# A decoder layer on one core: every stage laid out as [channel, token], norms summed over partitions, one address offset for matrix operands

## The chip, the cores and the metric

The kernel runs on 1 core of one Trainium2 chip. The metric is the device time of one execution in microseconds (us), median of the runs.

## What is computed

One layer (DEPTH 1), 1024 tokens, width 1024, float32:

```python
h = rmsnorm(x, g_mix); z = h @ w_in                 # 1024 x 7168, seven sections
y_rnn  = gelu(rnn_y) * rg_lru(causal_conv4(rnn_x))  # recurrence over the tokens
y_conv = conv_b * causal_conv3(conv_c * conv_x)
x = x + (sigmoid(gate_rnn) * y_rnn + sigmoid(gate_conv) * y_conv) @ w_out
g, u = split(rmsnorm(x, g_ffn) @ w_gate_up); x = x + (silu(g) * u) @ w_down   # inner width 2816
x = x + sigmoid(rmsnorm(x, g_ple) @ w_ple_gate) * (p @ w_ple)
return rmsnorm(x, g_final)
```

## The kernel before, in words

Each float32 operand of a product is kept as two halves (hi, lo) of 12 bits, and each 128x128 by 128x512 block takes three float32r matmuls. The large products use Strassen's scheme: seven products of quarter matrices, numbered 1 to 7, in place of eight. `mm` (L108) issues the three matmuls, `split` (L83) makes the halves: ScalarE casts (L85), VectorE subtracts (L86).

The stages, in order. **Start** (to 44 us): p @ w_ple in `ple` (L474), which stores `pe_d`, and the norm of x. **First stream** (to 638 us): the input projection as 28 pairs of channel blocks, with the recurrence (`rg` matmuls) and the convolutions. **Output projection** (`outer`, L336, to 716 us): product with w_out, added to x (`acc`, L433, line L435), stored as `x2_d`, normed. **Second stream** (to 1140 us): gate and up in 22 pairs. **Down projection** (to 1357 us): `outer` three times, added to x, stored as `x3_d`, normed. **Gate stage** (to the end): `gate` (L860) per block of 128 tokens, final norm, output.

A *stream* (L207) has channels on the partitions and tokens on the free axis. Its weights arrive as `part` tiles and become `wop` tiles (cast L250, subtraction L254) in pools `wp` (5 tiles) and `wq` (2); two products of each seven take `wq`. In a matmul `wop` is the loaded side (weights) and an operand made from the norm the moving side. There are seven such operands, B11, B21, T1, T2, B22, T3, -T4, of which B11 and B21 come from the first 512 tokens alone and the others from both halves. The first eight products use B11 and B21 only (`LEAD = 4` pairs); then the order is T2, T1, T3, T2, B22, T1, -T4.

Around the norms x is [token, channel], one tile per 128 tokens. `squares` (L115) lets ScalarE square a tile and sum along the free axis; `rstd` (L121) is a chain of small operations; rows are scaled (L144 on VectorE, L146 on ScalarE), and `transposed` (L148) turns each 128x128 block on TensorE (`tp`, L151), 64 blocks for each of the three norms. The reader of the bank applies the gain (L167, L169, L190, L192):

```python
def right_operands(r11, r21, xt, ss, gc, piece, held=0):
    ...
    scale_rows(xt, rstd(ss, 4), True)
    ...
            ps = transposed(xt, kk)
            t = r11[k // 2][:, k % 2]
            nc.vector.scalar_tensor_tensor(out=t, in0=ps, scalar=col(gc + kk), in1=t,
                                           op0=ALU.mult, op1=ALU.subtract)
            nc.scalar.activation(q[k // 2][:, k % 2], ps, AF.Copy, scale=col(gc + kk))
```

`r_late` tiles (L415) take the memory of the first half's x. Order on each engine is made at build time from priorities; `high_priority` and `sooner` move instructions forward, a negative offset back.

Memory, in bytes per partition, each tile rounded up to 32: constants `cp` 512 + 448 + 32 + 32 = 1024, then `ops` (seven operands of 16384), then `sm` (small tiles of the norms, 704 in all), then the pools of the stage. In a stream these are `w1`, `w2`, `ws` (multiples of 2048), `wp`, then `ev`, `e0` and behind them `wq`. `e0` holds four tiles of 512 floats in the second stream and of 516 in the first. In the gate stage half of one left operand lies in the place of x tiles (`op_in_x`, L845).

Of the kernel before, what the change touches and what calls it, by code (L numbers as in the profile page):

```python
# [25 lines left out]
# columns of the per-channel constants  # L26
C_W4, C_B4, C_BR, C_BI, C_LAM, C_W3, C_GM, C_GF, C_GP, NCST = 0, 32, 40, 48, 56, 64, 88, 96, 104, 112

# sections of the input projection
# [6 lines left out]
def kernel(ctx, tc, x, pT, w_in, w_gu, w_rg, w_out, w_down, w_pg, w_ple, cst, g_fin, out):  # L36
# [12 lines left out]
"""  # L49
# [12 lines left out]
    x2_d = tc.dram_tile([T, D], F32, name="x2_d")  # L62
    x3_d = tc.dram_tile([T, D], F32, name="x3_d")
    pe_d = tc.dram_tile([T, D], F32, name="pe_d")
# [8 lines left out]
    ident = cp.tile([P, P], F32, name="ident")  # L73
    make_identity(nc, ident)
    cs = cp.tile([P, NCST], F32, name="cs")
# [7 lines left out]
    def split(hi, lo, src):  # L83
        """hi + lo == src, each with 12 significant bits."""
        nc.scalar.copy(hi, src)  # L85
        nc.vector.tensor_sub(lo, src, hi.bitcast(F32))  # L86

    def op_of(pieces, name):
        """A quarter of a matrix, given as pieces [P, k, H], as an operand."""
        t = ops.tile([P, 2, 4, H], F32R, tag="op", name=name)  # L90
        k = 0
        for q in pieces:
            n = q.shape[1]
            split(t[:, 0, k:k + n], t[:, 1, k:k + n], q)
            k += n
        return t
# [18 lines left out]
    def squares(ss, n, piece, jp):  # L115
        junk = jp.tile([P, D], BF16, tag="junk", name="junk", bufs=1)
        nc.scalar.activation(junk[:, :piece.shape[1]], piece, AF.Square, accum_out=ss[:, n:n + 1])

    root = [None]  # the last square root, behind which other tables may be loaded

    def rstd(ss, nb):  # L121
        """(sum of the parts / D + EPS) ** -0.5, with one Newton step behind the table."""
        v = sm.tile([P, nb], F32, name="rv")
        total = ss[:, 0:nb]
        for n in range(nb, ss.shape[1], nb):
            add(v, total, ss[:, n:n + nb])
            total = v
# [12 lines left out]
    def scale_rows(xt, y, spread):  # L140
        """xt[b] *= y[:, b]; spread: VectorE takes its share."""
        for b in range(4):
            if spread:
                nc.vector.tensor_scalar_mul(xt[b], xt[b], y[:, b:b + 1])  # L144
            else:
                nc.scalar.activation(xt[b], xt[b], AF.Copy, scale=y[:, b:b + 1])  # L146

    def transposed(xt, kk):  # L148
        ps = bank("tp")
        for b in range(4):  # L150
            nc.tensor.transpose(ps[:, b * P:(b + 1) * P], xt[b][:, kk * P:(kk + 1) * P], ident)  # L151
        return ps

    def norm_half(xt, ss, gc, piece, spread):
# [3 lines left out]
        scale_rows(xt, rstd(ss, 4), spread)  # L158
        quarters = []
        for kh in range(2):  # L160
            q = [piece(), piece()]
            for k in range(4):
                kk = 4 * kh + k
                ps = transposed(xt, kk)
                dst = q[k // 2][:, k % 2]
                if spread and k % 2:
                    nc.vector.tensor_scalar_mul(dst, ps, col(gc + kk))  # L167
                else:
                    nc.scalar.activation(dst, ps, AF.Copy, scale=col(gc + kk))  # L169
# [3 lines left out]
    def right_operands(r11, r21, xt, ss, gc, piece, held=0):  # L173
# [4 lines left out]
        o = [op_of(r11, "b11"), op_of(r21, "b21")]  # L178
# [3 lines left out]
        scale_rows(xt, rstd(ss, 4), True)  # L182
        second = []
        for kh in range(2):
            q = [piece(), piece()]
            for k in range(4):
                kk = 4 * kh + k
                ps = transposed(xt, kk)
                t = r11[k // 2][:, k % 2]
                nc.vector.scalar_tensor_tensor(out=t, in0=ps, scalar=col(gc + kk), in1=t,  # L190
                                               op0=ALU.mult, op1=ALU.subtract)
                nc.scalar.activation(q[k // 2][:, k % 2], ps, AF.Copy, scale=col(gc + kk))  # L192
            second.append(q)
            o.append(op_of(r11, "t%d" % (kh + 1)))
        r12, r22 = second
        with tc.high_priority(offset=-160):
            t3 = op_of(each(sub, r12, r22, r12), "t3")
            o.append(op_of(r22, "b22"))
            o.append(t3)
            o.append(op_of(each(sub, r21, r21, r11), "t4"))  # L200
        return o, banks

# [1 line left out]
    def stream_pools(st):  # L204
        return {n: pool(st, n, bufs) for n, bufs in (("w1", 4), ("w2", 4), ("ws", 2), ("wp", 5), ("ev", 4), ("e0", LEAD), ("wq", 2))}

    def stream(pools, srcs, hops, banks, take, pump=lambda: None, ahead=2, early=0):  # L207
        """srcs: raw rows of each pair of channel blocks. take(n)(blk, half, psum, sb): takes
        psum + sb, block blk of pair n on token half half. pump(): called behind each product."""
        n_pairs = len(srcs)  # L210
        # Two pairs run interleaved, so that a sum in PSUM is read three products before it goes
        # on; the first pairs run the products of the first token half in front.
# [11 lines left out]
        def part(q, i, j):  # L224
            """Quarter A(i, j) of pair q."""
# [6 lines left out]
        def source(q, i):  # L232
            """What becomes the left operand of product i of pair q; the sums overwrite the quarters."""
# [102 lines left out]
    def outer(a, b, s1, nk, acc, after=lambda i: None, mid=lambda: None):  # L336
        """a, b: the four quarters of the operands as dicts of pieces (the sums overwrite them).
        after(i): called behind the results of product i."""
        def prep(i):
# [27 lines left out]
        for n, i in enumerate(order):  # L367
# [9 lines left out]
            for tb in range(4):  # L377
# [591 lines left out]
```

## Time and profile before

| what | value |
|---|---|
| median of 3 runs | 1460.45 us (1459.83 to 1461.36) |
| profiled execution | span 1458.2 us; a time of its own beside the span is not listed |
| mean granted TensorE clock | 0.997 of 2.4 GHz |
| busy: TensorE, VectorE, ScalarE | 99%, 74%, 54% of the span |
| matrix instructions | 6348, of these 192 transposes |

The span runs from the first to the last instruction. A busy TensorE is not one at its best pace: matmuls are pipelined, each lasts longer than the distance to the next one's start.

### The profile page before, as it was taken

How to read it: one execution, taken by the hardware profiler on the slowest of the kernel's cores; microseconds unless marked ns; L12 is line 12 of the kernel's file. 1: busy time of each engine (PE TensorE's matmuls, PEld its weight loads, DVE VectorE, ACT ScalarE, POOL GpSimd, SP SyncE). 2: the span in 40 equal slices, each digit the busy share in tenths (PEclk: the TensorE clock that was granted, in tenths of full speed). 3: DMA queues.
4: the chain of work that ended last, by engine and by line, in shares of the span. 5: the costliest groups of instructions: out<-in, count | busy, mean ns of one | idle time of the engine just before them, and what ended most of it. 6: DMA issues, size and time to landing. Idle time of an engine off the chain costs nothing.

```text
span 1458.2 us, 17521 instructions
## 1 busy us (share of the span) xinstructions
PE 1437.6 (99%) x6348; PEld 1176.0 (81%) x6348; DVE 1077.8 (74%) x1617; ACT 781.7 (54%) x1214; POOL 10.6 (1%) x20
## 2 busy tenths in 40 slices
PE   8999999999999999999999999999999999999997
PEld 6787888888888888878888888888888888888886
DVE  6989757965697669689796555555554899995854
ACT  7757746754775467545773333333333343346764
POOL 0000000000000000000000000000000000000000
PEclk9999999999999999999999999999999999999999
DMA  8321221122112211381522222222223761524431
GB/s 317 111 87 51 75 77 52 52 79 74 53 55 75 77 51 59 111 286 53 172 81 101 87 82 85 87 88 83 76 80 106 255 231 37 195 87 141 148 145 58
DMA packets 76742, 153.77 MB, mean 105 GB/s; under 512 B 7920, under 2 KB 7920, under 8 KB 76656
## 3 DMA queue, kind: packets, MB, share of 16 engines
q1 hardware_dynamic: 74768, 145.84, 29.9%
q0 software_dynamic: 1888, 6.82, 1.4%
q8 instruction: 50, 0.82, 0.2%
q14 instruction: 36, 0.29, 0.1%
HBM read 120.12 MB, written 32.51 MB: 105 GB/s over the span
## 4 chain that ended last, share of the span: by engine, by line
PE 90%; DVE 3%; DMA 3%; ACT 2%; issue 1%; SPq 0%; DVEq 0%; ACTq 0%
PE X L111 46%; PE Y L111 23%; PE Z L111 11%; PE pg L874 6%; PE rg L111 3%; PE tp L151 1%; DMA pe_d<-peo 1%; DMA xt<-x_d 1%; DMA xt<-in_x 0%; ACT b L85 0%; DVE a11b L100 0%; DMA act_d<-a 0%; DMA a<-m_d 0%; DMA m_d<-v 0%; DVE v L722 0%
## 5 line engine op out<-in xcount | busy, mean ns | idle before, releaser
L111 PE MATMUL X<-t,wop 128*128 128x512 f32 x1800 | 431.3, 393 | 0.0
L111 PEld LDWEIGHTS X<-t,wop 128*128 128x128 f32 x1800 | 338.2, 188 | 76.6 <-DVE wop L254 0.3
L250 ACT CAST wop<-part 128x512 fp32r<-128x512 f32 x300 | 183.7, 621 | 213.8 <-PE X L111 67.4
L254 DVE TENSOR_TENSOR wop<-part,wop 128x512 fp32r<-128x512 f32 x300 | 204.8, 689 | 89.0 <-ACT wop L250 87.8
L111 PE MATMUL Z<-b,wop 128*128 128x512 f32 x600 | 146.7, 393 | 0.4 <-ACT r_late L192 0.4
L111 PE MATMUL X<-b,wop 128*128 128x512 f32 x600 | 147.0, 393 | 0.0
L111 PE MATMUL Y<-b,wop 128*128 128x512 f32 x600 | 146.4, 393 | 0.0
L111 PE MATMUL Y<-t,wop 128*128 128x512 f32 x600 | 146.2, 393 | 0.0
L111 PEld LDWEIGHTS Z<-b,wop 128*128 128x128 f32 x600 | 112.5, 188 | 26.8 <-ACT r_late L192 0.9
L111 PEld LDWEIGHTS Y<-b,wop 128*128 128x128 f32 x600 | 112.8, 188 | 25.5
L111 PEld LDWEIGHTS Y<-t,wop 128*128 128x128 f32 x600 | 112.8, 188 | 25.2
L111 PEld LDWEIGHTS X<-b,wop 128*128 128x128 f32 x600 | 112.6, 188 | 24.6
L874 PE MATMUL pg<-b,a 128*128 128x512 f32 (+1 forms) x408 | 88.4, 378 | 0.0
L111 PE MATMUL X<-t,s 128*128 128x512 f32 x360 | 85.8, 392 | 0.0
L874 PEld LDWEIGHTS pg<-b,a 128*128 128x128 f32 x408 | 73.4, 188 | 14.6
L254 DVE TENSOR_TENSOR wop<-s,wop 128x512 fp32r<-128x512 f32 x50 | 34.5, 689 | 59.5 <-ACT wop L250 59.5
L111 PEld LDWEIGHTS X<-t,s 128*128 128x128 f32 x360 | 66.8, 188 | 13.9 <-DVE t L86 0.5
L271 ACT COPY p<-Y 128x512 f32<-128x512 f32 x50 | 29.2, 583 | 72.6 <-PE Y L111 72.6
L271 ACT COPY s<-X 128x512 f32<-128x512 f32 x50 | 29.2, 588 | 59.2 <-PE X L111 58.9
L271 ACT COPY u<-X 128x512 f32<-128x512 f32 x50 | 29.2, 584 | 49.6 <-PE X L111 49.1
L435 DVE TENSOR_TENSOR xt<-X,xt 128x512 f32<-128x512 f32 x64 | 43.8, 686 | 14.5 <-PE X L111 13.6
L111 PE MATMUL rg<-xo,rg_w 128*128 128x512 f32 x192 | 47.1, 393 | 0.1
(172 smaller groups left out, 1939.7 us busy)
## 6 DMA issues: line engine op xcount, KB each, us to landing
part<-in_w_in SPq DMA_DIRECT2D x120, 256.0 KB, 2.6
part<-in_w_gu SPq DMA_DIRECT2D x96, 256.0 KB, 2.7
act_d<-a SPq DMA_DIRECT2D x44, 256.0 KB, 2.4
x_d<-xt SPq DMA_DIRECT2D x32, 256.0 KB, 2.0
bc<-in_w_down SPq DMA_DIRECT2D x10, 512.0 KB, 5.8
a<-act_d SPq DMA_DIRECT2D x10, 512.0 KB, 5.9
xt<-in_x SPq DMA_DIRECT2D x8, 512.0 KB, 8.0
pe_d<-peo SPq DMA_DIRECT2D x16, 256.0 KB, 2.9
```

The costliest lines, as they stand in the source:

```text
L111: nc.tensor.matmul(ps, lhs(i), rhs(j), start=start and first and n == 0, stop=last and n == 2, skip_group_check=not start)
L151: nc.tensor.transpose(ps[:, b * P:(b + 1) * P], xt[b][:, kk * P:(kk + 1) * P], ident)
L250: nc.scalar.copy(t[:, 0], s)
L254: sub(t[:, 1], s, t[:, 0].bitcast(F32))
L271: nc.scalar.copy(t, ps)
L435: add(piece, ps, piece)
L874: nc.tensor.matmul(ps, left[k // 4](i, k % 4)[:, c:c + P], right[k // 4, dh][:, j, k % 4, r], start=n + k == 0, stop=n == 2 and k == 7)
```

## The change

x enters as [channel, token] and the result leaves so (the host transposes both); x, x2, pe and the gate stage follow. In `outer` the two operands swap sides, so the result has channels on the partitions. The sum of squares over channels is now over partitions: ScalarE squares each piece, VectorE adds the eight squares, four small matmuls with ones sum over partitions, and the root, once found, is spread to all partitions by four multiplications and four transposes. `x3_d` is gone, since x stays in memory until the end. The tiles' sizes are set so that `wp`, `wq`, `ops` and every frame start at the same offset modulo 512 bytes (`cp` 2048, `sm` 512, `wq` ahead of `ev`); all comments go.

```diff
+C_W4, C_B4, C_BR, C_BI, C_LAM, C_W3, C_GM, C_GF, C_GP, C_GL, NCST = 0, 32, 40, 48, 56, 64, 88, 96, 104, 112, 120
+    ones = cp.tile([P, P], F32, name="ones")
+    cs = cp.tile([P, 240], F32, name="cs")[:, 0:NCST]
...
+    class Sum:
+        def take(self, piece):
+            q = self.fr.pj.tile([P, self.width], F32, tag="sq" if self.t is not None else "s2", name="sq", bufs=2)
+            nc.scalar.activation(q, piece, AF.Square)
+            if self.t is None:
+                self.t = q
             else:
+                add(self.t, self.t, q)
+        def spread(self):
+            nb = self.width // P
+            ps = bank("sum")
+            for b in range(nb):
+                nc.tensor.matmul(ps[:, b:b + 1], self.t[:, b * P:(b + 1) * P], ones[:, 0:1], start=True, stop=True)
+            z = rstd(ps[:, 0:nb], nb)
+            zb = self.fr.pj.tile([P, nb, P], F32, tag="zb", name="zb", bufs=1)
+            for b in range(nb):
+                nc.vector.tensor_scalar_mul(zb[:, b], ones, z[:, b:b + 1])
+            rb = bank("rb")
+            for b in range(nb):
+                nc.tensor.transpose(rb[:, b * P:(b + 1) * P], zb[:, b], ident)
+            return rb[:, 0:self.width]
+    def scaled(out, piece, gc, c, rb):
+        nc.vector.scalar_tensor_tensor(out=out, in0=piece, scalar=col(gc + c), in1=rb, op0=ALU.mult, op1=ALU.mult)
...
-        scale_rows(xt, rstd(ss, 4), True)
+        r12, r22 = [piece(), piece()], [piece(), piece()]
+        for k in range(4):
+            nc.scalar.activation(r22[k // 2][:, k % 2], piece_of(xt, 1, 4 + k), AF.Copy, scale=col(gc + 4 + k))
+        for k in range(4):
+            t = r22[k // 2][:, k % 2]
+            nc.vector.scalar_tensor_tensor(out=t, in0=piece_of(xt, 1, k), scalar=col(gc + k), in1=t,
+                                           op0=ALU.mult, op1=ALU.subtract)
+        rb = total.spread()
+        for k in range(4):
+            scaled(r12[k // 2][:, k % 2], piece_of(xt, 1, k), gc, k, rb)
+            if k % 2:
+                sub(r12[k // 2], r12[k // 2], r11[k // 2])
+        for k in range(4):
+            t = r22[k // 2][:, k % 2]
+            nc.vector.scalar_tensor_tensor(out=t, in0=t, scalar=-1.0, in1=rb, op0=ALU.mult, op1=ALU.mult)
+            if k % 2:
+                add(r11[k // 2], r11[k // 2], r22[k // 2])
+        t2 = op_of(r11, "t2")
+        t1 = op_of(r12, "t1")
         with tc.high_priority(offset=-160):
+            t3 = op_of(r22, "t3")
+            b22 = op_of(each(add, r12, r12, r11), "b22")
+            t4 = op_of(each(sub, r21, r21, r11), "t4")
...
-        return {n: pool(st, n, bufs) for n, bufs in (("w1", 4), ("w2", 4), ("ws", 2), ("wp", 5), ("ev", 4), ("e0", LEAD), ("wq", 2))}
+        return {n: pool(st, n, bufs) for n, bufs in (("w1", 4), ("w2", 4), ("ws", 2), ("wp", 5), ("wq", 2), ("ev", 4), ("e0", LEAD))}
...
-                    mm(banks[tb], lambda s: ao[:, s, k, tb * P:(tb + 1) * P], lambda s: bo[:, s, k, :],
+                    mm(banks[cb], lambda s: bo[:, s, k, cb * P:(cb + 1) * P], lambda s: ao[:, s, k, :],
...
+        def finish(half, total, r=slice(0, H)):
+            rb = total.spread()
+            for j in range(4):
+                for c in (2 * j, 2 * j + 1):
+                    xr = piece_of(xt, half, c, r)
+                    scaled(xr, xr, C_GL, c, rb)
+                nc.sync.dma_start(out=rows2(out, half, j)[:, :, r], in_=xt[half][j][:, :, r])
...
+        for c in range(4, 8):
+            gate(0, c, left0, total)
+        for n in range(2):
+            r = slice(n * 256, n * 256 + 256)
+            part = Sum(fr, 256)
+            for c in range(8):
+                gate(1, c, left1, part, r, n == 1 and c == 7)
+                if n == 0 and c == 0:
+                    finish(0, total)
+            finish(1, part, r)
...
+    nc = bacc.Bacc("TRN2", target_bir_lowering=False, num_devices=1, dynamic_dma_scratch_size=8192)
```

The new `gate` takes one channel block and one token half: 24 matmuls, 512 columns wide in the first half, twice 24 of 256 columns in the second; VectorE multiplies by pe, adds to x, and the block's squares join the sum. `norm_half` now calls `spread` and then eight times `scaled` on VectorE.

## Rows read from the trace of the kernel before

**Rows 1.** The page, busy time (share of the span) and instructions per engine.
```profile
PE 1437.6 (99%) x6348; PEld 1176.0 (81%) x6348; DVE 1077.8 (74%) x1617; ACT 781.7 (54%) x1214; POOL 10.6 (1%) x20
```

**Rows 2.** Waits of TensorE: total us, times, longest us.
```profile
PE ple L111 <- ACT o_wple L85: 5.8, 2, 4.7
```

**Rows 3.** Windows, TensorE alone: stretch, width, busy (instructions), clock, DMA.
```profile
150.00:620.00 470.00, 470.00 (x2032) 1.00 0.21 69
760.00:1130.00 370.00, 370.00 (x1618) 1.00 0.27 89
1180.00:1330.00 150.00, 150.00 (x663) 1.00 0.41 136
1373.00:1404.00 31.00, 31.00 (x136) 1.00 0.36 136
1406.00:1443.00 37.00, 37.00 (x165) 1.00 0.29 112
1443.24:1449.16 5.92, 5.92 (x49) 1.00 0.22 89
```

**Rows 4.** The chain that ended last: start us, us, what.
```profile
83.19 8.40 PE X L111 x36
...
208.79 2.80 PE Z L111 x12
...
236.68 2.77 PE rg L111 x12
...
759.44 8.24 PE X L111 x36
```

**Rows 5.** The same chain, asked for 640 to 770 us.
```profile
704.49 1.31 PE tp L151 x12
```

**Rows 6.** Timeline of TensorE: the first stream's first product; the gate stage's transposes.
```profile
44.37 3.01 PE L111 MATMUL X<-b,wop 128*128 128x512 f32 x12
...
1368.56 3.65 PE L151 MATMUL tp<-ident,xt 128*128 128x128 f32 x32
```

**Rows 7.** Timeline of VectorE: start us, us, line, operation, count.
```profile
75.44 1.22 DVE L86 TENSOR_TENSOR t<-r,t 128x1024 fp32r<-128x1024 f32 x1
...
708.73 1.89 DVE L254 TENSOR_TENSOR wop<-part,wop 128x512 fp32r<-128x512 f32 x3
...
720.43 2.73 DVE L144 TENSOR_SCALAR xt<-xt,rz 128x1024 f32<-128x1024 f32 x4
...
732.05 2.06 DVE L190 SCALAR_TENSOR_TENSOR r<-tp,cs,r 128x512 f32<-128x512 f32 x3
...
738.11 2.35 DVE L86 TENSOR_TENSOR t<-r,t 128x1024 fp32r<-128x1024 f32 x2
...
753.89 1.22 DVE L86 TENSOR_TENSOR t<-r,t 128x1024 fp32r<-128x1024 f32 x1
```

**Rows 8.** Windows: stretch, width, busy of PE, PEld, DVE, ACT, POOL.
```profile
10.00:50.00 40.00, 36.99 (x178) 30.37 (x177) 32.45 (x65) 32.84 (x55) 0.00 (x0) 0.96 0.77 280
50.00:90.00 40.00, 40.00 (x175) 32.66 (x174) 38.76 (x68) 24.84 (x38) 0.00 (x0) 1.00 0.30 96
690.00:710.00 20.00, 20.00 (x106) 16.81 (x105) 12.66 (x26) 16.24 (x30) 0.00 (x0) 1.00 0.65 217
710.00:755.00 45.00, 44.52 (x210) 36.14 (x209) 43.54 (x60) 34.58 (x56) 0.00 (x0) 1.00 0.25 80
1330.00:1350.00 20.00, 20.00 (x104) 16.38 (x103) 6.83 (x15) 17.39 (x30) 0.00 (x0) 1.00 0.38 130
```

**Rows 9.** Timeline of the end: start us, us, engine, line.
```profile
1449.19 0.37 ACT L878 ACTIVATE pg<-pg 128x256 f32<-128x256 f32 x1 [0.98 <-PE pg L874]
...
1450.98 0.40 ACT L117 ACTIVATE junk<-fin 128x256 bf16<-128x256 f32 x1
...
1452.04 0.15 DVE L128 TENSOR_SCALAR rv<-rv 128x1 f32<-128x1 f32 x1
...
1453.24 0.49 DVE L894 TENSOR_SCALAR fin<-fin,rz 128x512 f32<-128x512 f32 x1
```

More of the change, by code (lines that the diff above doesn't have):

```diff
@@ L112, in mm, with piece_of, rstd @@
                              stop=last and n == 2, skip_group_check=not start)
-    def squares(ss, n, piece, jp):
-        junk = jp.tile([P, D], BF16, tag="junk", name="junk", bufs=1)
-        nc.scalar.activation(junk[:, :piece.shape[1]], piece, AF.Square, accum_out=ss[:, n:n + 1])
     root = [None]
-    def rstd(ss, nb):
+    def piece_of(xt, half, c, r=slice(0, H)):
+        return xt[half][c // 2][:, c % 2, r]
+    def rstd(total, nb):
         v = sm.tile([P, nb], F32, name="rv")
[L124 to L127, printed above, removed]
         nc.vector.tensor_scalar(out=v, in0=total, scalar1=1.0 / D, scalar2=EPS, op0=ALU.mult, op1=ALU.add)
@@ L138, in rstd, with __init__, norm_half @@
         return z
[L140 to L144, printed above, removed]
-            else:
[L146 to L158, printed above, removed]
+    class Sum:
+        def __init__(self, fr, width=H):
+            self.fr, self.width, self.t = fr, width, None
+        def take(self, piece):
[3 more added lines that the diff above has]
+                self.t = q
+            else:
+                add(self.t, self.t, q)
[14 more added lines that the diff above has]
+        nc.vector.scalar_tensor_tensor(out=out, in0=piece, scalar=col(gc + c), in1=rb, op0=ALU.mult, op1=ALU.mult)
+    def norm_half(xt, half, total, gc, piece):
+        rb = total.spread()
         quarters = []
@@ L162, in norm_half, with right_operands @@
             for k in range(4):
[L163 to L169, printed above, removed]
+                scaled(q[k // 2][:, k % 2], piece_of(xt, half, 4 * kh + k), gc, 4 * kh + k, rb)
             quarters.append(q)
         return quarters
-    def right_operands(r11, r21, xt, ss, gc, piece, held=0):
-        o = [op_of(r11, "b11"), op_of(r21, "b21")]
+    def right_operands(r11, r21, xt, total, gc, piece, held=0):
+        b11, b21 = op_of(r11, "b11"), op_of(r21, "b21")
         banks = [bank("X") for _ in range(held)]
@@ L409, in xs @@
         def xs(self, name="xt"):
-            return [(self.pa if b < 4 else self.pb).tile([P, D], F32, tag="x", name=name) for b in range(8)]
+            return [[p.tile([P, 2, H], F32, tag="x", name=name) for _ in range(4)] for p in (self.pa, self.pb)]
         def r(self):
@@ L754 @@
         load(a[1, 1], m_d, H, H)
-        load_x(x, xt)
+        load_x(xT, xt)
         load(b[1, 1], w_out, H, H)
-        ss = stats()
-        acc, after = residual(xt, ss, fr, True, x2_d)
+        sums = [Sum(fr), Sum(fr)]
+        acc, after = residual(xt, sums, True, x2_d)
         q_r = []
@@ L807 @@
         xt = fr.xs()
-        ss = stats()
+        sums = [Sum(fr), Sum(fr)]
         q_r = []
@@ L826 @@
             load(b[1, 1], w_down, r0 + rh, H)
-            acc, after = residual(xt, ss, fr, n == 2, x3_d)
+            acc, after = residual(xt, sums, n == 2, None)
             def after4(i):
@@ L843, in op_b, with op_in_r @@
                 right[j, dh] = op_of(raws[j, dh], "b")
-        def op_in_x(pieces, name):
-            t = [[fr.pa.tile([P, 2, H], F32R, tag="x", name=name) for _ in range(2)] for _ in range(2)]
+        def op_in_r(pieces, name):
+            t = [[fr.pr.tile([P, 2, H], F32R, tag="r", name=name) for _ in range(2)] for _ in range(2)]
             for n, q in enumerate(pieces):
@@ L900, with op_a, gate @@
-        left0 = op_a(q_r)
+        def op_a(pieces):
+            o = op_of(pieces, "a")
+            return lambda s, k: o[:, s, k]
+        def gate(half, c, left, total, r=slice(0, H), last=False):
+            dh, o = c // 4, (c % 4) * P
+            if (half, dh) not in pe:
+                t = pe[half, dh] = fr.pq.tile([P, 4, H], F32, tag="q", name="pe")
+                nc.sync.dma_start(out=t, in_=pe_d[4 * dh * P:(4 * dh + 4) * P, half * H:(half + 1) * H].rearrange("(k p) t -> p k t", p=P))
+            ps = bank("pg")[:, 0:r.stop - r.start]
+            for n, (i, j) in enumerate(((1, 0), (0, 1), (0, 0))):
+                for k in range(8):
+                    nc.tensor.matmul(ps, right[k // 4, dh][:, i, k % 4, o:o + P], left[k // 4](j, k % 4)[:, r],
+                                     start=n + k == 0, stop=n == 2 and k == 7)
+            t = nc.scalar.activation(ps, ps, AF.Sigmoid)
+            if last:
+                with tc.issue_after(t.ins):
+                    nc.scalar.sqrt(warm, warm)
+            pr, xr = pe[half, dh][:, c % 4, r], piece_of(xt, half, c, r)
+            nc.vector.tensor_mul(pr, ps, pr)
+            add(xr, xr, pr)
+            total.take(xr)
@@ L901 @@
+        def finish(half, total, r=slice(0, H)):
+            rb = total.spread()
+            for j in range(4):
+                for c in (2 * j, 2 * j + 1):
+                    xr = piece_of(xt, half, c, r)
+                    scaled(xr, xr, C_GL, c, rb)
+                nc.sync.dma_start(out=rows2(out, half, j)[:, :, r], in_=xt[half][j][:, :, r])
+        left0 = [op_a(q_r[0]), op_a(q_r[1])]
         op_b(0)
-        for b in range(2):
-            gate(b, 0, left0)
+        total = Sum(fr)
@@ new lines @@
+        for c in range(2, 4):
+            gate(0, c, left0, total)
+        left1 = [op_a(q_late[0]), op_in_r(q_late[1], "a")]
+        for c in range(4, 8):
+            gate(0, c, left0, total)
+        for n in range(2):
+            r = slice(n * 256, n * 256 + 256)
+            part = Sum(fr, 256)
+            for c in range(8):
+                gate(1, c, left1, part, r, n == 1 and c == 7)
+                if n == 0 and c == 0:
+                    finish(0, total)
+            finish(1, part, r)
```

180 lines of the change are left out of this document (47 added, 133 removed).

## The prediction

> **What bounds the kernel now.** The page comes first: TensorE is busy 99% of the span, and its longest wait of all, at the very start, is 5.8 us in total [rows 1, 2]. So the end moves only if TensorE gets less to issue, issues faster, or is made to wait. The second view is therefore the distance between matmul starts in each stage, from windows in which TensorE never rests. A window of W us counts each matmul whose 0.39 us touches it, so the distance is (W + 0.39) / count [rows 3]: 231.5 ns in the first stream, 228.9 in the second, 226.8 in the down projection, 230.8 in the gate stage while its left operand lies half in `ops` and half in the place of x, and 226.6 later in the same stage, when both sides are in `ops`. All have the same shape and granted clock 1.00, and all but the first are one kind of matmul after another.
>
> What differs is where the loaded side lies. With the byte counts in the section on the kernel, `ops` starts at some offset; `wp`, `wq` of the second stream and the x tiles come 704 bytes plus multiples of 2048 behind it, so 192 bytes off modulo 512; `wq` of the first stream has 4 x 2080 more in front and is 320 off. Difference 0 goes with 226.7, 192 with 228.9 to 231, 320 with 233 (a product of twelve in `wq`, Z, takes 2.80 us [rows 4]). In the first stream products in `wp` that follow such a one mostly keep its slower distance, which makes the mean 231.5. One row speaks against this reading: the `rg` matmuls have both sides in `wp`, difference 0, and still take 2.77 us for twelve, 231 ns [rows 4]; they run in short groups of six between products at 230 to 233.
>
> **The change part by part.**
>
> *One offset.* `cp` becomes 2048, `sm` loses `ss` (2 x 32) and `fss` (4 x 32) and is 512, `wq` moves ahead of `e0`: every loaded and moving operand then differs by a multiple of 512. If all run at 226.8: the first stream has 28 x 84 + 192 = 2544 matmuls; its first 120 run at about 229 and the rest at 231.5, so 0.3 + 2424 x 4.7 ns = 11.7 us. Second stream: 22 x 84 = 1848 x 2.1 ns = 3.9 us. Gate stage: 144 x 4 ns = 0.6, of which I take 0.2, since that window also holds the ends of groups. Together about 15.5 us; the ends are 0 (offset does not matter) and this. I take 15.3.
>
> Against it stands a rule. The Trainium skill, "TensorE: Matmul & The Clock Gate", section "Step-by-step: what each phase is for", says that TensorE reads the moving side and the next weights through two independent ports of SBUF, so that loading them takes no bandwidth from the running matmul. By it no offset could matter and this term would be 0, the sum 15.3 us higher. The trace does not agree: three distances at one shape and clock.
>
> *Transposes go, sums and spreads come.* Twelve transposes take 1.31 us on the path [rows 5], 0.11 each. A spread over 512 tokens issues four transposes (0.44) and four one-column matmuls, which no row shows; nearest are a transpose, 0.11, and a 512-column matmul, 0.23, and I take 0.2, nearer to the dearer because float32 is not split there: 1.3 us a spread, 0.9 to 1.4.
>
> *End of the down projection.* 32 transposes (3.5) go, one spread comes: -2.2 us. The work that VectorE takes over, four or eight additions and eight `scaled`, some 9 us, is hidden: VectorE is busy 6.8 of 20 us there [rows 8], and two products of 10.9 us follow.
>
> *Gate stage.* Before: 91.5 us, from 1357.69 to 1449.16, 32 transposes in 3.4 of them [rows 6]. After: 192 matmuls of 512 columns at 0.2268, 43.5, and 384 of 256 columns at 5.92 / 48 = 0.123 [rows 3], 47.2; a 256-column matmul costs 0.123, not half of 0.227, so the narrow pieces cost 3.7 us. With spreads for the second half's norm, the first half's end and half of the second's (3.3 us) that is 94.0: +2.5, between +1.5 and +4. Per block TensorE needs 5.4 us and VectorE three operations of 0.6: hidden.
>
> *The tail.* Before, from the last matmul (1449.16) to the end (1458.2): 9.0 us. Up to the square the same, ending 2.2 us behind the matmul [rows 9]. Then an addition (0.4), two ones matmuls (0.4), the root's chain (1.2, from 1452.04 to 1453.2 [rows 9]), two multiplications (0.5, between 0.15 and 0.49 each), two transposes (0.4), eight `scaled` of 256 columns: 0.66 at 512 [rows 7], halved with its fixed part 0.36, so 2.9. That is 8.0, and before 4.2 us lay between the end of the scaling (1453.96) and the end of the span: 12.1. +3, between +1.5 and +6; nothing covers it.
>
> *Start and first norm.* The first stream's first product starts at 44.37 [rows 6], behind the second half's transposes, which wait for buffers. Without them it can start when B11 is there: ones behind 72 `ple` matmuls at 26.3, root 28, spread 29.6, eight `scaled` to 35, B11's low half at 37: 7 us sooner. But VectorE must then make the other operands. From a run of operations a further one costs 0.60 (512 wide), 1.13 (1024 wide), 0.66 (scalar_tensor_tensor; also L144) [rows 7]. Added: 14 additions 8.4, zb 2.0, 16 `scaled` 10.6, four preparations 2.6, four more 1024-wide sums and differences 4.5; removed: 8 x L144 5.4, 4 x L167 2.8, 8 x L190 5.3. Net +14.6 us. VectorE is idle 7.5 us between 10 and 50, and 1.2 between 50 and 90 [rows 8]. -T4 is the last operand, complete at 76.7 [rows 7], and its product starts at 83.2 [rows 4]: slack 6.5. So 14.6 - 7 - 6.5 = +1 if VectorE decides, -7 if it does not. I take 0.
>
> *Norm between output projection and second stream.* TensorE alone: 64 transposes 7.0 and two spreads 2.6, -4.4, and 0.6 of a wait. VectorE: added 11 additions 6.6, zb 2.0, 16 `scaled` 10.6, preparations 2.6, wide sums 4.5; removed L144 2.7, L190 5.3. The eight that ScalarE did (L146, L169) are within the 16. Net +18. Idle: 7.3 of 20 us, then 1.5 of 45 [rows 8]. -T4 is done at 755.1 [rows 7], its product at 759.4 [rows 4]: slack 4.3. So 18 - 9 - 4.3 = +5 by VectorE, -5 by TensorE. VectorE is the fuller one: +3. Late next would be T2, then -T4, with TensorE's queue behind them.
>
> *No cost:* p and x arrive as many bytes as before; 32 stores and 8 loads of x3 and pe become fewer, and DMA queues are not in any wait above; the swap in `outer` leaves both sides in `ops`, as the 226.8 ns now; a smaller scratch only moves addresses.
>
> Sum: 1458.2 - 15.3 + 0 + 3 - 2.2 + 2.5 + 3 = 1449.2. The profiled execution's span stands 2.2 us below the median of the runs, 1460.45, so 1451.4; I say 1451.5.
>
> **The rivals.**
>
> *A, the distance does not follow the offset.* Then its 15.3 us stay and the costs remain: 1467. For it: the `rg` row, and the rule above, which by itself would give this time. Against it: the two windows of the gate stage, the same loop within 70 us, 230.8 and 226.6, where only the place differs. It decides (slower) once the gain is below 3 us. Chance 0.12.
>
> *B, VectorE starves TensorE at the two starts of the streams.* If nothing of the added work falls into idle time, the first start costs +8 and the second +14 in place of 0 and +3: 1470; with half of it 1461. For it: VectorE is busy 97% from 50 to 90 and from 710 to 755 [rows 8]. Against it: part of what it does there prepares weights of products that come later, and can slide. From 9 us more than I take the gain is gone. Chance 0.13.
>
> *C, VectorE's work is hidden.* -7 and -5 in place of 0 and +3: 1436.5. For it: the additions fall into the time in which x arrives. Chance 0.12.
>
> **How the numbers follow.** The forecast, 1451.5 with 1444 to 1458 from the ends of its terms, has 0.63. What a measurement of this kernel can tell from no change is about 0.2%, 2.9 us. Faster by more: 0.60 of the forecast, all of C, 0.03 of B: 0.75. Within: 0.03 of the forecast, 0.05 of B, 0.02 of A: 0.10. Slower: 0.05 of B, 0.10 of A: 0.15. The range 1438 to 1463 leaves out most of A, the dear half of B and half of C.
>
> **What would show it.** Windows of the same kind should give 226 to 228 ns in both streams; at 229 to 233, step one is wrong and A holds. TensorE's waits should name VectorE at T2 or -T4 for a few us at the starts (over 12 in all: B; none: C). The gate stage should last 94 us, with 256-column pieces at 0.123, and the tail 12. The prediction fails above all if float32 ones matmuls cost far over 0.2 us or sit in TensorE's queue ahead of products while the root is still being found.

## The result: 2.8% slower, and the profile after

The changed kernel takes 1502.37 us (median of 4 runs, 1497.34 to 1506.45) where the kernel before took 1460.9 beside it: ratio 1.0279, 95% interval 1.0255 to 1.0302. 1451.5 was forecast, and 1463 was the upper end of the range. The profiled execution spans 1500.4 us (before 1458.2), with a mean granted clock of 0.976.

From the page of the changed kernel: instructions per engine as in [rows 1], then the clock in 40 slices of 37.5 us.

```profile
PE 1433.3 (96%) x6420; PEld 1188.4 (79%) x6420; DVE 1134.0 (76%) x1712; ACT 738.1 (49%) x1118; POOL 10.6 (1%) x20
...
PEclk9799999999999999999899999999999999999998
```

TensorE is no longer busy throughout. Its waits, to be held against [rows 2] (total us, times, longest us):

```profile
PE sum L156 <- DVE sq L149: 13.2, 4, 7.3
PE rb L163 <- DVE zb L160: 12.9, 5, 6.4
PE ple L112 <- DVE o_wple L87: 7.4, 2, 5.4
PE X L112 <- DVE wop L264: 6.6, 2, 6.3
PE X L112 <- ACT s L281: 3.9, 1, 3.9
PE Y L112 <- DVE wop L264: 3.7, 1, 3.7
PE X L112 <- ACT wop L260: 3.3, 1, 3.3
PE pg L862 <- ACT sq L145: 2.6, 1, 2.6
```

The two longest did not exist before: ones matmuls (`sum`) that wait for the last addition of squares, and the transposes that spread the root (`rb`) that wait for the root's chain. Where they stand is seen in the timeline of TensorE, here the two starts (start us, us, what, in brackets the idle time ahead and what ended it; [rows 6] has the first product at 44.37):

```profile
40.25 0.95 PE L156 MATMUL sum<-ones,sq 128*128 128x1 f32 x8
47.63 1.09 PE L163 MATMUL rb<-ident,zb 128*128 128x128 f32 x4 [6.43 <-DVE zb L160]
55.01 5.49 PE L112 MATMUL X<-b,wop 128*128 128x512 f32 x12 [6.29 <-DVE wop L264]
...
83.80 5.52 PE L112 MATMUL X<-t,wop 128*128 128x512 f32 x16 [3.87 <-ACT s L281]
...
731.85 1.86 PE L156 MATMUL sum<-ones,sq 128*128 128x1 f32 x8 [7.26 <-DVE sq L149]
733.58 6.84 PE L112 MATMUL X<-b,wop 128*128 128x512 f32 x22
...
760.94 4.54 PE L112 MATMUL X<-t,wop 128*128 128x512 f32 x12 [3.28 <-ACT wop L260]
...
780.12 4.40 PE L112 MATMUL Y<-t,wop 128*128 128x512 f32 x12 [3.75 <-DVE wop L264]
```

A product of twelve takes 2.7 us at full clock. The 5.49 behind a gap is half clock (granted 0.50 from 55 to 60 us), the 4.54 partly so (0.62 over it). Not every gap is followed by it: behind 1.01 us of idle time at 90.33 us a product of twelve takes 3.01. The same in the gate stage:

```profile
1432.97 1.02 PE L156 MATMUL sum<-ones,sq 128*128 128x1 f32 x8 [0.79 <-DVE sq L149]
1435.61 0.33 PE L163 MATMUL rb<-ident,zb 128*128 128x128 f32 x1 [1.61 <-DVE zb L160]
...
1460.36 0.77 PE L156 MATMUL sum<-ones,sq 128*128 128x1 f32 x4 [2.44 <-DVE sq L149]
1462.73 0.48 PE L163 MATMUL rb<-ident,zb 128*128 128x128 f32 x1 [1.60 <-DVE zb L160]
```

What did come as forecast is the distance between matmul starts. Windows of TensorE as in [rows 3]:

```profile
150.00:620.00 470.00, 469.52 (x2070) 1.00 0.21 64
800.00:1140.00 340.00, 340.00 (x1502) 1.00 0.26 81
```

(470 + 0.39) / 2070 = 227.2 ns (0.5 us of that window was idle), then 226.6, where 231.5 and 228.9 stood.

Windows of VectorE (width, busy, instructions, clock, DMA), from 10 us to the first stream's product of -T4, and from the end of the first stream to the second stream's product of -T4, first before the change:

```profile
10.00:83.03 73.03, 64.35 (x112) 0.98 0.53 189
633.79:759.28 125.49, 114.25 (x150) 1.00 0.40 135
```

and after it:

```profile
10.00:103.16 93.16, 83.58 (x149) 0.85 0.45 156
642.98:784.32 141.34, 133.29 (x182) 0.94 0.35 120
```

Both stretches grow (by 20.1 and 15.9) by about what VectorE's busy time grows (19.2 and 19.0); its idle time in them hardly shrinks (8.7 to 9.6, and 11.2 to 8.1). A longer stretch also takes in work that is not new: of the first 19.2 us about 4 are weights and operands that fall into it. Yet -T4's operand is not what its product waits for. Its last low half, in either start of the changed kernel:

```profile
88.39 1.22 DVE L87 TENSOR_TENSOR t<-r,t 128x1024 fp32r<-128x1024 f32 x1
...
777.02 2.35 DVE L87 TENSOR_TENSOR t<-r,t 128x1024 fp32r<-128x1024 f32 x2
```

It is complete 13.6 us ahead of its product at 103.16, and 5.0 ahead of the one at 784.32; before the change it was 6.5 and 4.3. TensorE stands earlier: of the 20.1 us, 10.6 lie ahead of the first product (55.01 for 44.37), and the rest are waits and half clock between it and -T4.

The span by stage, from the same timelines; each stage ends where the next begins:

| stage | before | after | difference | the prediction's step |
|---|---|---|---|---|
| to the first stream's -T4 | 83.03 | 103.16 | +20.1 | 0 |
| rest of the first stream | 550.76 | 539.82 | -10.9 | -11.7 |
| output projection to the second stream's -T4 | 125.49 | 141.34 | +15.9 | +3 |
| rest of the second stream | 384.53 | 381.06 | -3.5 | -3.9 |
| down projection to the first gate matmul | 213.72 | 214.74 | +1.0 | -2.2 |
| gate stage to its last matmul | 91.63 | 108.16 | +16.5 | +2.5 |
| tail | 9.0 | 12.2 | +3.2 | +3 |

### The profile page after: what moved, and what is told of

Read it like the earlier page. It is cut to its first block, busy times and chain, and to the rows that moved or that the text cites. A ratio compares the mean times of both kernels' runs of the same rounds, so it can differ in the third digit from the quotient of the medians.

```text
span 1500.4 us, 17540 instructions
## 1 busy us (share of the span) xinstructions
PE 1433.3 (96%) x6420; PEld 1188.4 (79%) x6420; DVE 1134.0 (76%) x1712; ACT 738.1 (49%) x1118; POOL 10.6 (1%) x20
## 4 chain that ended last, share of the span: by engine, by line
PE 87%; DVE 8%; DMA 2%; ACT 2%; issue 1%; SPq 0%; DVEq 0%; ACTq 0%
PE X L112 44%; PE Y L112 22%; PE Z L112 10%; PE pg L862 6%; PE rg L112 3%; DVE t L87 1%; DVE sq L149 1%; PE ple L112 1%; DVE wop L264 1%; PE sum L156 1%; DVE xt L441 1%; DMA xt<-x_d 0%; DVE b L87 0%; DMA a<-m_d 0%; DMA wple<-in_w_ple 0%
## 5 line engine op out<-in xcount | busy, mean ns | idle before, releaser
L862 PE MATMUL pg<-a,b 128*128 128x256 f32 (+1 forms) x576 | 97.7, 333 | 3.2 <-ACT sq L145 2.6
L862 PEld LDWEIGHTS pg<-a,b 128*128 128x128 f32 x576 | 87.6, 202 | 11.9 <-ACT sq L145 3.0
L112 PE MATMUL X<-s,t 128*128 128x512 f32 x360 | 84.0, 391 | 0.6 <-DVE t L87 0.6
L112 PEld LDWEIGHTS X<-s,t 128*128 128x128 f32 x360 | 67.3, 188 | 14.9 <-DVE t L87 1.0
L145 ACT ACTIVATE sq<-xt 128x512 f32<-128x512 f32 (+1 forms) x72 | 41.5, 583 | 67.1 <-DVE xt L441 27.4
L149 DVE TENSOR_TENSOR sq<-sq 128x512 f32<-128x512 f32 (+1 forms) x63 | 39.6, 629 | 12.7 <-ACT sq L145 11.2
```

The source lines that it names most:

```text
L145: nc.scalar.activation(q, piece, AF.Square)
L149: add(self.t, self.t, q)
L862: nc.tensor.matmul(ps, right[k // 4, dh][:, i, k % 4, o:o + P], left[k // 4](j, k % 4)[:, r], start=n + k == 0, stop=n == 2 and k == 7)
```

## The experiments

Three stretches lose far more than was forecast: the two starts and the gate stage. Theory 1: the ones matmuls and the transposes of the root stand in TensorE's queue ahead of products that are ready, and half clock follows some of the gaps. Theory 2 (rival B): VectorE's added work makes operands and weights late, wherever these matmuls stand. Theory 3 came up on the way: the place in memory of the first stream's weights. All times are medians; the interval is that of the ratio to the kernel before, run beside each.

| run | us | ratio, 95% interval |
|---|---|---|
| before, offset alone | 1445.63 | 0.9884 to 0.9921 |
| changed, old offsets | 1516.99 | 1.0369 to 1.0400 |
| changed, gate norms later | 1501.30 | 1.0258 to 1.0293 |
| changed, gate norms in two steps | 1491.06 | 1.0201 to 1.0232 |
| changed, second half's spread late | 1502.68 | 1.0267 to 1.0305 |
| changed, frame of five | 1495.98 | 1.0232 to 1.0263 |
| changed, zb in squares (control) | 1505.83 | 1.0276 to 1.0327 |
| changed, no additions | 1488.18 | 1.0174 to 1.0208 |
| both repairs (five, two steps) | 1489.86 | 1.0182 to 1.0216 |
| both repairs, spread late | 1503.61 | 1.0273 to 1.0322 |
| both repairs, additions on GpSimd | 1493.45 | 1.0212 to 1.0246 |
| both repairs, squares first | 1492.34 | 1.0200 to 1.0237 |
| both repairs, no additions | 1472.73 | 1.0069 to 1.0099 |
| both repairs, sum from the first square | 1486.81 | 1.0160 to 1.0192 |
| before, offset, 30 idle additions | 1463.56 | 1.0008 to 1.0036 |

### The offset, alone and taken back

```diff
+    for pool_, n in ((cp, 256), (sm, 80)):
+        nc.vector.memset(pool_.tile([P, n], F32, name="pad", bufs=1)[:, 0:1], 0.0)
...
-        return {n: pool(st, n, bufs) for n, bufs in (("w1", 4), ("w2", 4), ("ws", 2), ("wp", 5), ("ev", 4), ("e0", LEAD), ("wq", 2))}
+        return {n: pool(st, n, bufs) for n, bufs in (("w1", 4), ("w2", 4), ("ws", 2), ("wp", 5), ("wq", 2), ("ev", 4), ("e0", LEAD))}
...
-    nc = bacc.Bacc("TRN2", target_bir_lowering=False, num_devices=1)
+    nc = bacc.Bacc("TRN2", target_bir_lowering=False, num_devices=1, dynamic_dma_scratch_size=8192)
```

> The kernel before with only the offset of its operands changed: all loaded and moving tiles start at the same offset modulo 512; norms, transposes and layouts stay. If the distance between matmul starts follows the offset (the one step of the prediction that the trace after seems to bear out), both streams' windows go from 231.5 and 228.9 to about 227 ns and the time falls by 15 us or somewhat more: 1441 to 1446. If the distance does not follow the offset (rival A), windows and time stay: 1458 to 1463, and the short distances of the changed kernel have another cause.

The reverse, in the changed kernel: `cs` without its padding, `wq` last, 192 bytes more in `sm`; the smaller DMA scratch stays, so it is not what the two runs share.

> The changed kernel with the operands' offsets put back to the differences they had before (wp 192, wq of the first stream 320 modulo 512 against ops), all else as changed. If the offset is worth what the sum gave it, the time rises by 15 to 20 us over the changed kernel: about 1517 to 1522, the streams' windows back to 229 to 232 ns, and the stalls at the starts as they are. If offsets do nothing: 1502.

-15.6 us alone (beside 1461.27), and +14.6 when taken back: in both runs what the expectation gives if the distance follows the offset. Windows of both streams, first with the offset alone, then in the changed kernel with the old offsets:

```profile
150.00:620.00 470.00, 470.00 (x2076) 1.00 0.23 75
750.00:1120.00 370.00, 370.00 (x1634) 1.00 0.28 90
```

```profile
150.00:650.00 500.00, 499.85 (x2158) 1.00 0.23 73
850.00:1180.00 330.00, 330.00 (x1444) 1.00 0.27 90
```

226.6 and 226.7 ns; 231.9 and 228.8. In the last kernel `ops` itself lies 32 bytes further modulo 512 (`cp` is 1568 bytes), and the down projection, both sides in `ops`, still takes 226.4 (576 matmuls in the 130 us from 1210). The rule weighed in the prediction, two independent read ports (the Trainium skill, "TensorE: Matmul & The Clock Gate", "Step-by-step: what each phase is for"), lets no offset matter; the measurement decides against that use of it.

### The gate stage: both matmuls of a norm must be put off, apart

```diff
-                if n == 0 and c == 0:
-                    finish(0, total)
-            finish(1, part, r)
+                if c == 2:
+                    finish(*((0, total) if n == 0 else (1, parts[0], slice(0, 256))))
+            parts.append(part)
+        finish(1, part, r)
```

> The changed kernel with the norms of the gate stage's first half and of the second half's first 256 tokens asked for two blocks of 256 columns (some 11 us) later, so that their ones matmuls stand in TensorE's queue behind products that are ready. Theory 1 (the queue's order: ones matmuls that wait for VectorE and ScalarE block the products behind them, and half clock follows each gap): the two stalls of about 5 us and their half-clock matmuls in the gate stage go, 8 to 12 us less than the changed kernel: 1490 to 1494. Theory 2 (VectorE has too much work, or 256-column pieces are slow by themselves): at most 2 us less.

No gain (1.1 us): theory 1 missed. Its timeline shows why:

```profile
1438.55 0.95 PE L156 MATMUL sum<-ones,sq 128*128 128x1 f32 x8
1442.10 0.47 PE L163 MATMUL rb<-ident,zb 128*128 128x128 f32 x1 [2.60 <-DVE zb L160]
```

`sum` waits no more, but `rb` follows it directly and waits for the whole root. So `spread` was cut in two: `begin` holds the ones matmuls, the root and `zb`, and `finish` what follows.

```diff
+                if c == 1:
+                    parts[n][1].begin()
+                if c == 4:
+                    finish(*parts[n])
+            parts.append((1, part, r))
+        finish(1, part, r)
```

> The changed kernel with the gate stage's norms in two steps: the ones matmuls of a finished part are put behind two blocks of the next part, and the four (or two) transposes that spread the root three blocks later still, so that sum and rb both stand in TensorE's queue behind products that are ready, and the root is made in between. Putting both later together changed nothing, the wait only went from sum to rb. If the queue's order is what the gate stage lost (theory 1), both stalls of the stage and the half-clock matmuls behind them go now: 9 to 13 us less, 1489 to 1493. If VectorE or the narrow matmuls set the stage's end: 0 to 3 us.

```profile
1434.19 0.95 PE L156 MATMUL sum<-ones,sq 128*128 128x1 f32 x8
1435.01 8.88 PE L869 MATMUL pg<-a,b 128*128 128x256 f32 x72
1443.72 0.60 PE L170 MATMUL rb<-ident,zb 128*128 128x128 f32 x4
```

11.3 us, as theory 1 said, and neither gap is left; 256 columns go at 8.88 / 72 = 0.123, the price that the prediction had. The clock in two windows of all engines (PE first, clock behind POOL), in the changed kernel and with two steps:

```profile
1425.00:1440.00 15.00, 12.59 (x77) 11.57 (x76) 9.41 (x23) 5.40 (x8) 0.00 (x0) 0.89 0.08 29
1460.00:1475.00 15.00, 13.04 (x89) 12.98 (x90) 7.51 (x23) 4.48 (x8) 0.00 (x0) 0.77 0.22 71
```

```profile
1425.00:1440.00 15.00, 15.00 (x114) 14.38 (x113) 7.41 (x22) 6.92 (x12) 0.00 (x0) 1.00 0.01 1
1460.00:1475.00 15.00, 15.00 (x127) 15.00 (x127) 10.19 (x30) 5.72 (x13) 0.00 (x0) 1.00 0.22 71
```

### The first start: where the first weights lie

In the changed kernel the first weights are cast at 48.25 us, before the change at 23.62. The diff has a line that neither the cut above nor the prediction took up: the first frame's pool of quarters went from five tiles to two. The stream's pools take the frame's place; `wp` lies 20480 to 40960 bytes behind its start. Five quarters of 8192 covered that and are free early. With two, x's second half (from 16384) and the squares lie there, and the norm reads them to the end. `zb` had to share a buffer to make room:

```diff
-            zb = self.fr.pj.tile([P, nb, P], F32, tag="zb", name="zb", bufs=1)
+            zb = self.fr.pj.tile([P, nb, P], F32, tag="sq" if self.fr.first else "zb", name="zb", bufs=2 if self.fr.first else 1)
...
-        fr = Frame(st, "p0", 2)
+        fr = Frame(st, "p0", 5)
```

> The changed kernel with five buffers in the first frame's pool of quarters, as before the change (the change made them two); for the room, zb of that frame takes its buffer from the squares. The first stream's weights tiles wop then lie over buffers that are free early and not over x's second half and the squares. Theory 3 (place): in the changed kernel the casts of the first weights wait until the norm has read x's second half; with five buffers they run from about 25 us, the first product starts at 45 to 48 us and not 55.0, and the product of -T4 8 us or more before 103.2: 8 to 15 us less in all, 1488 to 1495. Theory 2 (VectorE's added work alone makes operands late): the first product may start sooner, but that of -T4 stays at 101 to 104, and the time within 3 us of 1502.

The control has the line of `zb` and keeps two quarters.

> The control for the run with five buffers: the changed kernel in which only zb of the first frame takes its buffer from the squares, with two buffers of quarters as changed. Under every theory the start stays as in the changed kernel, first product at 55 within 1.5 us, and the time at 1502 within 3 us; anything else would be the price of the shared buffer.

Timeline of ScalarE with five, and of TensorE:

```profile
23.59 1.91 ACT L260 CAST wop<-part 128x512 fp32r<-128x512 f32 x3 [3.95 <-DMA part<-in_w_in]
```

```profile
47.56 1.86 PE L156 MATMUL sum<-ones,sq 128*128 128x1 f32 x8 [9.55 <-DVE sq L149]
52.86 0.45 PE L163 MATMUL rb<-ident,zb 128*128 128x128 f32 x1 [3.44 <-DVE zb L160]
52.96 5.04 PE L112 MATMUL X<-b,wop 128*128 128x512 f32 x12
```

The casts are early again, and the product of -T4 starts at 97.58 (changed kernel 103.16, control 103.98). The run takes 6.4 us less than the changed kernel and 9.9 less than the control, which came out 3.5 above the changed kernel, just outside its bound. The expected first product at 45 to 48 did not come: ahead of it now stands `sum`, waiting 9.55 us for VectorE.

### The second start: order, chain or load

First the order: the spread of the second half at a lower priority.

```diff
-        rb = total.spread()
+        with tc.high_priority(offset=-90):
+            rb = total.spread()
```

> The changed kernel with the second half's spread (its ones matmuls, root and transposes) in right_operands given a lower priority, so that it is put into the engines' queues after the first products and not ahead of them. Theory 1 (queue order): the first product of each stream starts sooner (55.0 to below 50; the 7.3 us stall ahead of the second stream goes), and 10 to 15 us are gained: 1487 to 1492. Theory 2 (VectorE's added work makes the operands late wherever the ones matmuls stand): the first products start sooner, but the product of -T4 starts no sooner than now (103.2 and 784.3 us), the wait only moves to T2 and -T4, and the time changes by less than 3 us: 1499 to 1505, or rises when the spread itself becomes what T2 waits for.

> The kernel with both repairs, and in both starts the second half's spread at a lower priority, so that its transposes come behind five products and not behind one. If the queue's order still costs time at the starts, 4 to 8 us less than with both repairs alone: 1477 to 1482. If VectorE's work decides there (what the run with the late spread alone suggests), the product of -T4 stays within 2 us of that kernel in both streams, and the time within 3 us: 1482 to 1488.

In the changed kernel the second stream's first product came at 731.3 and not 733.6, but its -T4 at 784.0 and not 784.3, as theory 2 had it. The run tests the order only in part: most of `sum` still stood ahead of that product and waited 6.2 us (7.3 before). With both repairs the late spread cost 13.8 us (-T4 at 107.2 for 97.7, and 796.1 for 781.7): T2 and -T4 hang on `rb`, and VectorE idles until it comes (busy 30.6 of the 40 us from 50 to 90, with both repairs 38.0). Neither theory had expected that.

Then the load, by leaving out the additions (`self.t = q` in `take`).

> The changed kernel without the additions of squares: every norm takes the sum from its last square alone, so the result is not the norm, and VectorE has 63 operations (some 40 us in all) less. Theory 2 (VectorE's work decides at the second start): the product of -T4 of the second stream starts 6 us or more sooner against the last product of the output projection (that start took 131 us from its end of the first stream, before the change 125), and in the gate stage each wait of sum gets shorter by about the 0.7 us of one addition: 10 to 16 us less in all, 1486 to 1492. Theory 1 (queue order) alone: the ones matmuls still wait for the last square and the root, the gate stage keeps its three waits of 4 to 5 us, the second start keeps a wait of 5 us or more ahead of its first product, and less than 6 us are gained.

(The 131 us in this text is a slip; the changed kernel takes 141.3.) It took 132.3, 9.1 less, while the gate stage kept its length (108.2 to 109.2 us up to its last matmul), its waits now mostly at `rb`: theory 2 at the start, theory 1 in the gate stage. With both repairs:

> The changed kernel with both repairs: five buffers in the first frame (zb there takes the place of a finished sum, so that the squares keep both of theirs), and the gate stage's norms in two steps. If the place of the first weights (some 6 to 8 us) and the queue's order in the gate stage (11 us) are independent losses, they add: 1483 to 1487. If the gain of five buffers was an accident of the squares' order, 1490 to 1493.

> The kernel with both repairs without the additions of squares (each norm from its last square alone, so that the result is not the norm): the bound for all that can be had by taking them off VectorE. Theory 2: about 9 us less at the second start and 3 to 5 at the first than with both repairs, 1471 to 1476; what then stays above the kernel with only the offset changed (1446) is the rest of VectorE's added work, the narrow matmuls and the tail. If the additions were harmless with both repairs in place: within 3 us of it.

The repairs do not add: 1489.86 is only 1.2 below the two steps alone. -T4 of the first stream comes at 97.7, as with five quarters alone, so that gain was no accident of the shared buffer. But of the 4.2 us by which this is sooner than with two steps alone, 1.2 are left at the second stream's -T4: half of the rest goes in the first stream behind -T4 (541.3 us for 539.8), half in the second start (142.7 for 141.3). Why stays open. Without additions 1472.73, as expected. That takes away load and chain together. To part them, the additions stay and their result is not used (`add(q, q, self.t)`); or `take` gets a high priority; or it uses `nc.gpsimd.tensor_add`; or idle additions go into a kernel that has no new norm, 14 ahead of its scaling of rows and two at each of eight pieces behind:

```diff
+        for n in range(14 if dead[0] is not None else 0):
+            add(dead[0], r11[n % 2][:, 0], r21[n % 2][:, 0])
...
+                for n in range(2 if dead[0] is not None else 0):
+                    add(dead[0], r21[n][:, 0], r21[n][:, 1])
```

> The kernel with both repairs, in which every norm takes its sum from its first square alone, while all additions of squares are still done (their results are used by nothing, so that the result is not the norm). The load on VectorE is that of the kernel with both repairs (1490), the chain of additions ahead of the sum is gone as in the kernel without additions (1473). If the load decides: 1484 to 1491, and from the end of the first stream to the second stream's -T4 140 us or more, as with both repairs (142.7). If the chain decides: 1471 to 1478, and 131 to 135 us there.

> The kernel with both repairs, with squares and their additions put ahead of other work in the queues of ScalarE and VectorE, nothing left out. If the chain to the sum decides, the ones matmuls' waits ahead of the first products (9.5 us and 7.3 us) shrink by half or more and 5 to 10 us are gained: 1480 to 1485. If VectorE's load decides, the waits move to the products behind, and the time stays within 4 us of 1490.

> The kernel before with only the offset changed (1445.6), with 30 additions of 512 columns, some 18 us, put into VectorE's queue at the start of the second stream alone, their result used by nothing: the norm, the transposes and the queues of the other engines are those of the kernel before. If VectorE's load decides there (rival B, nothing of it fits into idle time): from the end of the first stream to the second stream's -T4 126 us become 138 to 143, and the time 1457 to 1463. By the prediction's account (9 us of idle time and 4.3 us of slack take it up): +5, 1450 to 1452. If only the new norm's chain costs: 1445 to 1448.

> The kernel with both repairs, with the 63 additions of squares on GpSimd in place of VectorE. Theory 2 (VectorE's work decides the second start): 6 to 10 us less than with both repairs, 1475 to 1480, most of it between the end of the first stream and the second stream's product of -T4. Against it: an addition on GpSimd has no row; if one takes over 1.2 us, a chain of seven comes later than on VectorE, the ones matmuls wait longer, and the time is equal or up to 10 us more.

Windows of VectorE from the end of the first stream to the second stream's -T4 (width, busy, instructions): both repairs; no additions; sum from the first square; offset alone; offset and 30 idle additions.

```profile
639.01:781.73 142.72, 134.24 (x184) 0.93 0.36 121
```

```profile
634.58:766.97 132.39, 126.02 (x170) 0.97 0.39 131
```

```profile
638.47:781.51 143.04, 134.68 (x184) 0.92 0.35 121
```

```profile
621.32:747.43 126.11, 115.10 (x151) 1.00 0.39 134
```

```profile
621.52:767.09 145.57, 134.12 (x184) 0.94 0.34 116
```

The width follows the busy time: without the chain but with the load it stays at 143.0, and in a kernel without any of the new norm 19.0 us of idle additions cost 19.5 (the run 17.9). Putting the squares first gained nothing. What TensorE waits for, with the idle additions (two lines), and with the sum from the first square:

```profile
PE tp L154 <- DVE xt L147: 6.4, 1, 6.4
PE Y L113 <- DVE a L792: 5.7, 1, 5.7
```

```profile
PE X L112 <- DVE X L194: 8.3, 1, 8.3
```

The idle additions stand ahead of the scaling of rows and of later sums in VectorE's queue, which is busy without a break from 697.4 to 745 us; the 7.2 us of idle time ahead of that (677.5 to 697.4) are as long as with the offset alone (7.4). This is the load, at its full price; the expectation (138 to 143 us) was still too low. The run with the first square is the weaker test, since it frees `sum` but not the first product: that now waits for the small memset that reserves its bank (L194), which stands in VectorE's queue behind the additions (at 728.37 us with both repairs, at 699.99 without additions). Putting this memset first was not tried. It is not what the idle additions cost: there the memset comes at 697.5 and the first product at 705.7, and -T4 is late all the same.

GpSimd gave no relief (the run is 3.6 us above both repairs). The stretch there is 147.8 us, and VectorE is as busy with 16 instructions fewer:

```profile
637.12:784.91 147.79, 133.27 (x168) 0.93 0.34 115
...
722.54 2.32 DVE L87 TENSOR_TENSOR b<-r,b 128x1024 fp32r<-128x1024 f32 x1
...
730.26 1.39 POOL L149 TENSOR_TENSOR sq<-sq 128x512 f32<-128x512 f32 x1 [2.55 <-ACT sq L145]
...
730.53 1.67 DVE L200 SCALAR_TENSOR_TENSOR r_late<-xt,cs,r_late 128x512 f32<-128x512 f32 x1
```

The operation at 730.53 takes 0.74 elsewhere, the one at 722.54 takes 1.22; beside an addition of GpSimd they take 1.67 and 2.32. Nine operations of the stretch are longer by 0.5 to 1.1 us in this way, 8.4 in all. The Trainium skill, "Perfetto Trace Analysis", "Optimizing Scalar/DVE Operations", says that GpSimd shares a read port with VectorE, so that moving work between the two may not help; the row agrees.

## Why the prediction was wrong, step by step

- **One offset, -15.3**: right. -15.6 measured alone, -14.4 in the two streams of the changed kernel. (Its terms, 11.7, 3.9 and 0.2, add up to 15.8 and not to "about 15.5".) Rival A falls; the `rg` products that spoke for it also take 2.72 us per twelve now, so their 2.77 [rows 4] was not a pace of their own. Their two sides lie at difference 0 in both kernels, so the difference alone does not explain that 2.77; what does stays open.
- **Start and first norm, 0: +20.1.** The added work was sized about right (14.6 forecast, VectorE's busy time grew by 19.2). The step that failed is the path: -T4's operand was taken for what sets the start, with "7 us sooner" and "slack 6.5" to take the work up. The slack grew to 13.6 us and bought nothing, since TensorE stands earlier. The start came no sooner: its weights had lost their early place (5.6 to 6.4 us by the run with five), and `sum` and `rb` stood ahead of the first product. The additions are worth 4.3 us (-T4 at 93.4 for 97.7). The rest, about half, was not taken apart. That it is the rest of VectorE's work is argued from its busy time (with both repairs it is busy all of the 16.5 us up to the first `rb` at 52.4), not shown; in every run with five quarters the first product still starts right behind that `rb`, so theory 1 was never tested there by itself.
- **Norm between output projection and second stream, +3: +15.9.** Net work +18 was right (19.0). "18 - 9 - 4.3" failed. Of the 9 us of idle time 3.1 were taken (11.2 to 8.1), and with the idle additions none: work that stood behind the idle time in VectorE's queue did not fill it. The slack of 4.3 is still there (5.0); TensorE waits at `sum` and at the weights (7.3, 3.3 and 3.7 us) instead. This is rival B, beyond its dear end (+14), though not at the operands T2 and -T4 where it was to show. How much of it the place of `sum` and of the memset adds to the load was not parted.
- **End of the down projection, -2.2: +1.0.** -1.8 up to the start of its last product, near the -2.2; then the first gate matmul waits 2.6 us, by the profile for a square on ScalarE, which was not forecast and not tried. Without additions that wait is absent, yet the stretch is no shorter (215.4 us); why stays open.
- **Gate stage, +2.5: +16.5.** The matmuls were sized right. "VectorE three operations of 0.6: hidden" holds for the blocks and not for the norms: TensorE stood behind `sum` and `rb`. This is the condition that the prediction ended on, ones matmuls "in TensorE's queue ahead of products while the root is still being found"; it was named and given no price. Two steps give 11.3 back; 97.0 of the stage's 108.2 us are left, against 94.0 forecast, and no run took that rest apart.
- **The tail, +3**: right, 12.2 against 12.1.

No version of the change beat the kernel before. The offset alone does, by 15.6 us.

## What to carry to other kernels

Between two fixed points of the critical engine's work, take the helper engine's busy time and its idle time; work added there costs its full length where what it waits for, or its place in that engine's queue, puts it behind the idle time. Then look for what the critical engine really waits for: an operand that comes later, but still before its product, is not it. A small matmul that needs another engine's answer belongs in the queue only where that answer is due, and a pair with a chain in between needs two places. Read every line of a diff that sizes a pool: it decides whose memory the next stage must wait for.

## What the runs showed of the hardware

- Loading and moving sides at equal offset modulo 512 bytes: 226.6 ns between matmuls; 192 apart: 228.8; the stream with 192 and 320: 231.9. It holds in both directions and both kernels; other differences were not run.
- A GpSimd addition of 512 columns takes 1.29 to 1.54 us at the second start (mean of all 49: 1.47) where VectorE's pitch is 0.60, and an operation of VectorE beside it up to 1.1 us longer.
- Four ones matmuls of one column (eight records in the trace) take 0.95 us at full clock, near the 0.2 each of the estimate.
